# Expert weights in 8 KB rows, and the token rows of six expert pairs fetched by indirect DMA

## The chip, the cores and the metric

The kernel runs on one core of one Trainium2 chip. The metric is device time in microseconds (us). The kernel before has a median of 1703.13 us over three runs (1701.49 to 1704.36).

## The reference

One layer (DEPTH = 1) over 512 latent tokens of width 1024 with 256 context tokens. In fp32 it computes, for `x`:

```python
h = modulate(x, norm1_g, sh_a, sc_a)             # RMSNorm with shift and scale
# three mixers on h: HGRN2 recurrence both ways, gated depthwise conv, grouped-query attention;
# gated projections summed, then w_out
x = x + g_a * y_lat
h = modulate(x, norm2_g, sh_f, sc_f)             # RMSNorm with shift and scale
aff = softmax(h @ router_w)                      # 512 x 16 experts
w_sel, idx = top_k(aff.T, 64)                    # each expert chooses 64 tokens
xs = h[idx]                                      # 16 x 64 x 1024
hid = silu(xs @ w_gate) * (xs @ w_up)            # each expert has 3 weights of 1024 x 1024
ys = (hid @ w_down) * w_sel
x = x + g_f * scatter_add(ys, idx)
out = rmsnorm(x, final_norm_g)
```

The expert weights are 16 x 3 x 4.19 MB, 201 MB in fp32, each read once.

## The kernel before, in words

Up to about 1190 us the kernel computes the mixers, the residual `x1` (four tiles of 128 tokens by 1024) and the router. The change leaves that part alone but for the order of columns in the router and in two small vectors. Attention already runs in program order there; no line of it is in the diff.

The expert stage takes two experts at a time, eight pairs, numbered 0 to 7 here as in the code. `one_hot` (line 1027) makes the 0/1 matrix of a pair: 128 slots, 64 for each expert, over 512 tokens; `ohs` is this matrix with each token's 1/rms (`ss2`) in it. `gather` (line 1039) multiplies `x1` by `ohs` on TensorE, so that the 128 chosen token rows come out transposed and normalised in `xT`, eight column blocks of 128; VectorE and ScalarE apply scale and shift when they evict them. `pair_chunks` (line 1092) multiplies a quarter of a 1024-row weight by the two halves of `xT`, one expert in each half of the partitions. Silu and the product give `hid`; it is transposed to `hT` and multiplied by `w_down`. `weights` (line 1056) fetches each slot's router weight with the same one-hot, `by_slot` (line 1067) transposes the one-hot, and `scatter` (line 1077) adds the results of the pair before to `acc` by matmul.

The order on TensorE is the program's own (a manual schedule). In pair `pr` it is: gate and up chunks of `pr`, gather of `pr + 1`, slot weights, scatter of `pr - 1`, transposes of `hid`, one-hot transposes, down chunks. In pair 0 its own gather stands between the chunks. VectorE, ScalarE and GpSimd are ordered by the planner.

The weights come through SyncE's (SP's) queue in the order of use. A load is one quarter of one expert's matrix, 256 rows of 1024, 1 MB (`wsrc`, line 941); a partition gets two rows that lie 128 rows apart, so two pieces of 4 KB. The last `w_down` pair is loaded by columns instead (`LASTC`), ten loads with pieces of 1 KB or less. The first 24 loads go to 24 slots as these come free; after that the slots are a ring of 20 (`RING`), and load number i waits until TensorE has used load i - 20. `refill` issues what has become possible after each chunk. `early` (line 1103) is the gather of pair 0, two column blocks at a time.

Of the kernel before, what the change touches and what calls it, by code (L numbers as in the profile page):

```python
# [51 lines left out]
def body(tc, x, ctx, cvec, ada_w, ada_b, ada_b0, n1g, n2g, hgn, convw, qg, kg, fng, w_in, w_pa, w_pb, w_pc, w_out,  # L52
# [20 lines left out]
    sc0 = const.tile([128, KC], F32, name="sc0")  # L73
    iota = const.tile([128, 64], F32, name="iota")
    vecs = const.tile([128, 8, 8], F32, name="vecs")
# [94 lines left out]

    last_w = []


# [547 lines left out]

    def column(src, put):
        p = pl.tile([128, KC], F32, name="tp")
        for k in range(KC):
            pe.matmul(p[:, k:k + 1], src[:, k * 128:(k + 1) * 128], ones[:, 0:1], start=True, stop=True)
        put(p)

    def ada_more():

        if not todo:  # L730
            return
        g, k = todo.pop(0)
        w = wraw()
        sp.dma_start(w, ada_w[k * 128:(k + 1) * 128, g * 2048:(g + 1) * 2048])
        if k == 0:
            accs[g] = acp.tile([128, 2048], F32, name="acc")
            ab_r = acp.tile([1, 2048], F32, name="abr")
            act.dma_start(ab_r, ada_b[:, g].rearrange("o j n -> o (j n)"))
            dve.tensor_scalar(accs[g], w, sc0[:, k:k + 1], None, op0=OP.mult)
            dve.tensor_add(accs[g][0:1], accs[g][0:1], ab_r)  # L740
        else:
            dve.scalar_tensor_tensor(accs[g], w, sc0[:, k:k + 1], accs[g], op0=OP.mult, op1=OP.add)
        if k == KC - 1:
            lo, hi = accs[g][:, 0:1024], accs[g][:, 1024:2048]
            if g == 1:
                later.append(lambda: gate_rows(lo))
                later.append(lambda: column(hi, lambda p: dve.tensor_copy(ab2[:, 1], p)))
            else:
                later.append(lambda: column(lo, lambda p: dve.scalar_tensor_tensor(ab2[:, 0], p, 1.0, vecs[:, 1],
                                                                                  op0=OP.add, op1=OP.mult)))  # L750
                later.append(lambda: column(hi, lambda p: dve.tensor_copy(gfc, p)))
# [100 lines left out]
    ss2 = xp.tile([128, 4], F32, name="ss2")  # L852
    aff = xp.tile([128, 4, NE], F32, name="aff")

# [16 lines left out]
    def partial_logits(j2, t):  # L871
        tp = pr_.tile([128, 2, 2, 128], F32, name="tp", bufs=2)
        for kk in range(2):
            for i in range(2):
                pe.transpose(tp[:, kk, i], x1[:, t + i, j2 * 256 + kk * 128:j2 * 256 + kk * 128 + 128], ident)
        xT = wo.tile([128, 2, 2, 128], F32, name="xT", bufs=3)
# [6 lines left out]
    for j2 in range(4):  # L883
# [4 lines left out]
        for t in range(0, 4, 2):  # L888
# [14 lines left out]
            if (j2, t) == (3, 0):  # L903
                preload(ssp[:, 0, 3:4])
    partial_logits(*pend.pop())
    dve.tensor_reduce(ss2, ssp, axis=AX.X, op=OP.add)
    act.activation(ss2, ss2, AF.Sqrt, scale=1.0 / D, bias=eps)
    dve.reciprocal(ss2, ss2)
    pl4 = pr_.tile([128, 4, NE], F32, name="tp", bufs=2)
    for t in range(2):  # L910
# [20 lines left out]
    ma, ma_e = opn("ma", side="right", reuse_waits="tile")  # L931
    wsel = sm.tile([128, NE // 2], F32, name="wsel")
    slot = sm.tile([128, 4, NE], F32, name="slot")
    mx = sm.tile([128, 4], F32, name="rmx")
# [7 lines left out]
    for pr in range(NE // 2):  # L942
        pair = (2 * pr, 2 * pr + 1)
        for kk in range(4):
            for mat in (w_gate, w_up):
                wsrc += [mat[e, kk * 256:kk * 256 + 256].rearrange("(a p) f -> p a f", p=128) for e in pair]
        if pr < NE // 2 - 1:
            for kk in range(4):
                wsrc += [w_down[e, kk * 256:kk * 256 + 256].rearrange("(a p) f -> p a f", p=128) for e in pair]
# [7 lines left out]
    def more(n):  # L957
        for src in wsrc[len(loaded):len(loaded) + n]:
            i = len(loaded)
            name = ORDER[i] if i < len(ORDER) else ring[(i - len(ORDER)) % RING]  # L960
            t = slots[name].tile(list(src.shape), F32, name="mw")
            sp.dma_start(t, src)
            loaded.append(t)

# [58 lines left out]
    pm, pm_e = opn("pm", space=PSUM, bufs=1)  # L1023
    xs = {}
    hot = {}

    def one_hot(pr):
# [5 lines left out]
        dve.tensor_tensor(oh.rearrange("p t (e c) -> p t e c", e=2), slot[:, :, e0:e0 + 2, None].to_broadcast(shape),  # L1033
                          iota[:, None, None, :].to_broadcast(shape), op=OP.is_equal)
        ohs = ma.tile([128, 4, 2 * CAP], F32, name="ohs")
        dve.tensor_mul(ohs, ohf, ss2[:, :, None].to_broadcast([128, 4, 2 * CAP]))
        hot[pr] = oh, ohf, ohs

    def gather(pr, k0, p, on_act):

        ohs = hot[pr][2]
        if pr not in xs:
            xs[pr] = ma.tile([128, KC, 2 * CAP], F32, name="xT")
        xT = xs[pr]
        n = p.shape[1]
        for i in range(n):
            for t in range(4):
                pe.matmul(p[:, i], x1[:, t, (k0 + i) * 128:(k0 + i + 1) * 128], ohs[:, t], start=t == 0, stop=t == 3)  # L1048
        for k in range(k0, k0 + n):
            if on_act:  # L1050
                act.activation(xT[:, k], p[:, k - k0], AF.Identity, scale=ab2[:, 0, k:k + 1], bias=ab2[:, 1, k:k + 1])
            else:
                dve.tensor_scalar(xT[:, k], p[:, k - k0], ab2[:, 0, k:k + 1], ab2[:, 1, k:k + 1], op0=OP.mult,  # L1053
                                  op1=OP.add)

    def weights(pr):

        e0 = 2 * pr
        ohf = hot[pr][1]
        pw = ps.tile([128, NE], F32, name="d")  # L1060
        for t in range(4):
            pe.matmul(pw, ohf[:, t], aff[:, t], start=t == 0, stop=t == 3)
        for e in range(2):
# [39 lines left out]
    def early(k0):  # L1103
        gather(0, k0, ps.tile([128, 2, 128], F32, name="d"), False)

    with tc.manual_schedule(engines={mybir.EngineType.DVE}):
        one_hot(0)
        early(0)
    waiting = None
    for pr in range(NE // 2):  # L1110
# [3 lines left out]
        for kk in range(4):  # L1114
            if kk and pr == 0:
                early(2 * kk)
            for po in (pg, pu):
                pair_chunks(kk, po, xs[pr])
            if pr == 0 and kk == 3:
                one_hot(1)  # L1120
            if last and kk == 0:
                scatter(*waiting, 1, lambda t: ps.tile([128, 1, 512], F32, name="d"))
                weights(pr)
                oT_t = by_slot(pr)
            if last and kk == LATE:
# [20 lines left out]
        if not last and waiting:  # L1146
            scatter(*waiting, 2, lambda t: pm.tile([128, 2, 512], F32, name=("pg", "pu")[t // 2]))
        hT = mb.tile([128, KC, 128], F32, name="hT")
        for h4 in range(2):
            tp = ps.tile([128, 4, 128], F32, name="d")  # L1150
            for i in range(4):
                k = 4 * h4 + i
                pe.transpose(tp[:, i], hid[:, k * 128:(k + 1) * 128], ident)
            act.activation(hT[:, 4 * h4:4 * h4 + 4], tp, AF.Copy)
        if 0 < pr < NE // 2 - 1:
            oT_t = by_slot(pr)
            if pr + 2 < NE // 2:
                one_hot(pr + 2)
        py = pm.tile([128, 2, 512], F32, name="py")
# [4 lines left out]
        if pr == 0:  # L1164
# [13 lines left out]
        waiting = pr, oT_t, yH, yL  # L1178


    sfp = sm.tile([128, 4, len(LASTC)], F32, name="sfp")
    sf = sm.tile([128, 4], F32, name="sf")
# [50 lines left out]
def layout(inp):  # L1233
# [23 lines left out]
    a["w_out"] = f["w_out"][0]  # L1257
    a["router"] = f["router_w"][0].reshape(8, 128, 16).transpose(1, 0, 2)
    a["w_gate"] = f["w_gate"][0]
# [12 lines left out]
    a["sin_d"] = np.sin(ang).astype(np.float32).reshape(4, 128, 32).transpose(1, 0, 2)  # L1272
    a["iota_d"] = np.tile(np.arange(1, 65, dtype=np.float32), (128, 1))
    return {k: np.ascontiguousarray(v) for k, v in a.items()}
# [24 lines left out]
```

## Time and profile before

| | |
|---|---|
| median of three runs | 1703.13 us |
| the profiled execution: its time, its span | 1698.42 us, 1696.6 us |
| TensorE busy (PE) | 1607.2 us, 95% |
| VectorE, ScalarE, GpSimd busy | 767.9, 527.7, 150.7 us |
| moved by DMA | 305.52 MB |
| loads of expert weights | 194 on SP's queue |

The span runs from the first to the last instruction, and the profiled execution's time is 1.8 us longer. PE is TensorE's matmul and PEld its weight load, which overlaps it. A busy PE is not a PE at its peak. The DMA share is the mean busy share of 16 DMA engines; it can exceed 1 a little because packets overlap. For a DMA, the profile gives the issue and the time to landing.

### The profile page before, as it was taken

The numbers are of one execution on the slowest core, as the hardware profiler recorded it, in microseconds if no ns is written. First come the engines' busy times: TensorE is split into PE (matmuls) and PEld (weight loads), VectorE is DVE, ScalarE is ACT, GpSimd is POOL, SyncE is SP. The second block draws the span as 40 slices with busy tenths as digits, with TensorE's granted clock in tenths as the row PEclk, the third lists the DMA queues.
The fourth block names the chain that finished last, engine by engine and source line by source line (L and its number), as shares of the span: only waits on it lengthen the run. The fifth ranks groups of instructions, "written<-read, shape, count | busy, mean of one in ns | idle before, by whom it ended". The sixth has DMA issues, their size and how long they took to land.

```text
span 1696.6 us, 23600 instructions
## 1 busy us (share of the span) xinstructions
PE 1607.2 (95%) x9896; PEld 1207.7 (71%) x9896; DVE 767.9 (45%) x1173; ACT 527.7 (31%) x934; POOL 150.7 (9%) x142
## 2 busy tenths in 40 slices
PE   6999999999998899899999999999799999999996
PEld 4889898988898788788788888889244344444444
DVE  6364655556545666655646524343411222122124
ACT  4433324334225656654323223233010010011004
POOL 0021212222000000000000100110000000000005
PEclk9999999999999999999999999999899999999998
DMA  9410211122222000100555622348789999999995
GB/s 294 118 41 25 63 38 50 38 75 70 80 80 75 26 25 26 44 33 26 182 191 178 209 85 75 124 148 349 315 320 402 382 409 409 409 409 409 409 395 167
DMA packets 166287, 305.52 MB, mean 180 GB/s; under 512 B 6562, under 2 KB 115618, under 8 KB 164130
## 3 DMA queue, kind: packets, MB, share of 16 engines
q1 hardware_dynamic: 162624, 301.66, 48.9%
q10 hardware_dynamic: 3556, 2.35, 0.4%
q8 instruction: 78, 1.28, 0.3%
q14 instruction: 29, 0.24, 0.0%
HBM read 301.89 MB, written 2.10 MB: 179 GB/s over the span
## 4 chain that ended last, share of the span: by engine, by line
PE 83%; DVE 9%; ACT 5%; issue 2%; POOL 0%; DMA 0%; ACTq 0%; SPq 0%; DVEq 0%; POOLq 0%
PE d L185 14%; PE d L187 14%; PE d L186 14%; PE pg L1099 6%; PE pu L1099 6%; PE py L1099 6%; PE py L1048 3%; PE lv L304 2%; PE tp L647 2%; PE tp L632 2%; DVE wl L91 1%; PE mi L333 1%; PE sc L617 1%; PE sc L618 1%; ACT wh L90 1%
## 5 line engine op out<-in xcount | busy, mean ns | idle before, releaser
L185 PE MATMUL d<-hH,wh 128*128 128x512 f32 x640 | 257.2, 402 | 0.0
L187 PE MATMUL d<-hH,wl 128*128 128x512 f32 x640 | 253.4, 396 | 0.0
L186 PE MATMUL d<-hL,wh 128*128 128x512 f32 x640 | 252.4, 394 | 0.0
L91 DVE TENSOR_TENSOR wl<-raw,wh 128x2048 fp32r<-128x2048 f32 (+1 forms) x78 | 157.8, 2022 | 192.0 <-ACT wh L90 191.8
L90 ACT ACTIVATE wh<-raw 128x2048 fp32r<-128x2048 f32 (+1 forms) x78 | 128.9, 1652 | 218.2 <-PE d L186 167.4
L187 PEld LDWEIGHTS d<-hH,wl 128*128 128x128 f32 x640 | 121.0, 189 | 24.9
L185 PEld LDWEIGHTS d<-hH,wh 128*128 128x128 f32 x640 | 120.8, 189 | 22.3 <-issue 1.6
L186 PEld LDWEIGHTS d<-hL,wh 128*128 128x128 f32 x640 | 121.1, 189 | 21.3 <-issue 0.2
L1099 PE MATMUL pg<-mw,xT 128*64 128x512 f32 x512 | 115.6, 593 | 2.0 <-DVE xT L1053 2.0
L1099 PE MATMUL pu<-mw,xT 128*64 128x512 f32 x512 | 115.3, 592 | 0.0
L1099 PE MATMUL py<-mw,hT 128*64 128x512 f32 x448 | 97.7, 594 | 0.1
L315 POOL TENSOR_TENSOR kk<-kk,tt 128x384 f32<-128x384 f32 x56 | 77.0, 1376 | 190.8 <-DVE tt L317 143.6
L1099 PEld LDWEIGHTS pu<-mw,xT 128*64 128x64 f32 x512 | 36.7, 137 | 73.1 <-issue 72.8
L1099 PEld LDWEIGHTS pg<-mw,xT 128*64 128x64 f32 x512 | 36.1, 137 | 72.2 <-issue 68.8
L185 PE MATMUL d<-wh,hH 128*128 128x256 f32 x288 | 84.1, 292 | 0.0
L187 PE MATMUL d<-wh,hL 128*128 128x256 f32 x288 | 81.7, 284 | 0.0
L186 PE MATMUL d<-wl,hH 128*128 128x256 f32 x288 | 81.6, 283 | 0.0
L1140 DVE TENSOR_TENSOR hid<-hid,pu 128x1024 f32<-128x1024 f32 x8 | 9.8, 1221 | 154.4 <-PE pu L1099 148.0
L187 PE MATMUL d<-brh,wl 128*128 128x512 f32 x192 | 75.6, 396 | 2.6 <-DVE wl L91 2.6
L185 PE MATMUL d<-brh,wh 128*128 128x512 f32 x192 | 75.8, 396 | 1.7 <-ACT wh L90 1.5
L186 PE MATMUL d<-brl,wh 128*128 128x512 f32 x192 | 75.7, 396 | 0.0
L1099 PEld LDWEIGHTS py<-mw,hT 128*64 128x64 f32 x448 | 31.5, 137 | 60.8 <-issue 59.7
(354 smaller groups left out, 2998.1 us busy)
## 6 DMA issues: line engine op xcount, KB each, us to landing
mw<-in_w_gate_dram SPq DMA_DIRECT2D x64, 1024.0 KB, 18.2
mw<-in_w_up_dram SPq DMA_DIRECT2D x64, 1024.0 KB, 18.5
mw<-in_w_down_dram SPq DMA_DIRECT2D x62, 1024.0 KB, 17.4
raw<-in_w_in_dram SPq DMA_DIRECT2D x38, 1024.0 KB, 5.1
raw<-in_ada_w_dram SPq DMA_DIRECT2D x16, 1024.0 KB, 4.9
raw<-in_w_in_dram SPq DMA_DIRECT2D x24, 512.0 KB, 3.8
adaw<-in_ada_w_dram SPq DMA_DIRECT2D x8, 512.0 KB, 8.5
raw<-in_ada_w_dram SPq DMA_DIRECT2D x8, 512.0 KB, 7.8
```

What stands on the lines that cost most here:

```text
L90: act.activation(hi, src, AF.Copy)
L91: dve.tensor_sub(lo, src, hi)
L185: pe.matmul(p, lh(k), rh(k), start=k == 0, stop=False)
L186: pe.matmul(p, lh(k), rl(k), start=False, stop=False)
L187: pe.matmul(p, ll(k), rh(k), start=False, stop=k == KC - 1)
L304: pe.matmul(p[:, c], kc[:, c * 128:(c + 1) * 128], q_mix, start=True, stop=True)
L315: pool.tensor_mul(kb[:, :, 1], kb[:, :, 1], tb[:, :, 0, 0:1].to_broadcast([128, n2, m]))
L333: pe.matmul(pv[:, i], kt[:, i], v[:, c], start=True, stop=True)
L632: pe.transpose(tp[:, t], e[:, (t0 + t) * 128:(t0 + t + 1) * 128], ident)
L647: pe.matmul(av[hh * 64:hh * 64 + 64, i], va[:, t, g * 64:g * 64 + 64], pts[hh][:, t], start=t == 0, stop=t == 5)
L1048: pe.matmul(p[:, i], x1[:, t, (k0 + i) * 128:(k0 + i + 1) * 128], ohs[:, t], start=t == 0, stop=t == 3)
L1099: pe.matmul(dst[64 * e:64 * e + 64, hf_], src[:, k, 64 * e:64 * e + 64], wt[e][:, k2, hf_ * 512:hf_ * 512 + 512], start=k == 0, stop=k == ...
```

## The change

- **Weight loads.** A quarter's 256 rows are laid out so that partition p gets rows 2p and 2p + 1, which follow each other in memory: one piece of 8 KB instead of two of 4 KB. The pieces of the last `w_down` pair stay.
- **Order of columns.** With that layout a column block of a weight's rows holds every second row of 256. All that meets them is permuted to match by `every2`: the gather, the transposes of `hid` (but for the last pair), the router's transposes, the modulation vectors, `norm2_g` and the router weight.
- **Token rows.** `x1` is stored to a DRAM buffer `xd` by four DMAs on SP. From pair 2 on the gather by matmul is gone. `weights` now also multiplies the one-hot by the token's number and its 1/rms (`facts`), and so yields the index of each slot's token (`which`) and its 1/rms (`norm`). `fetch` reads the 128 rows from `xd` with an indirect DMA on GpSimd's queue and scales them on VectorE. `turn_rows` transposes them in eight blocks on TensorE and evicts them half on VectorE, half on ScalarE.
- **Order.** In pair `pr` TensorE now does: gate and up chunks, `turn_rows(pr + 1)`, slot weights of `pr + 2`, transposes of `hid`, scatter of `pr - 1`, one-hot transposes of `pr + 1`, down chunks. Pairs 0 and 1 keep the gather. `fetch(pr + 2)` comes at the end of pair `pr`; `fetch(2)` after the first chunks of pair 1. The fetched rows, `hid` and `yt` share one buffer.

```diff
+    def every2(v, k):
+
+        o = k // 2 * 256 + k % 2
+        return v[:, o:o + 255:2]
...
+    facts = xp.tile([128, 4, NE + 2], F32, name="aff")
+    aff = facts[:, :, :NE]
+    dram, dram_e = opn("xd", space=bass.MemoryType.DRAM)
+    xd = dram.tile([S, D], F32, name="xd")
...
+    for t in range(4):
+        sp.dma_start(xd[t * 128:(t + 1) * 128], x1[:, t])
...
+    pool.tensor_copy(facts[:, :, NE:NE + 1], iota[:, 64:68, None])
+    pool.tensor_copy(facts[:, :, NE + 1:NE + 2], ss2[:, :, None])
...
-                wsrc += [mat[e, kk * 256:kk * 256 + 256].rearrange("(a p) f -> p a f", p=128) for e in pair]
+                wsrc += [mat[e, kk * 256:kk * 256 + 256].rearrange("(p a) f -> p (a f)", p=128) for e in pair]
...
+            if len(src.shape) == 2:
+                t = t.rearrange("p (a f) -> p a f", a=2)
...
+    def evict(xT, p, k, on_act):
+        if on_act:
+            act.activation(xT[:, k], p, AF.Identity, scale=ab2[:, 0, k:k + 1], bias=ab2[:, 1, k:k + 1])
+        else:
+            dve.tensor_scalar(xT[:, k], p, ab2[:, 0, k:k + 1], ab2[:, 1, k:k + 1], op0=OP.mult, op1=OP.add)
+
+    def pick(pr, k0, p, on_act):
+
+        xT, ohs = xs[pr]
         n = p.shape[1]
         for i in range(n):
             for t in range(4):
+                pe.matmul(p[:, i], every2(x1[:, t], k0 + i), ohs[:, t], start=t == 0, stop=t == 3)
+        for i in range(n):
+            evict(xT, p[:, i], k0 + i, on_act)
+
+    def fetch(pr):
+
+        xg = mb.tile([128, D], F32, name="hid")
+        pool.indirect_dma_start(xg, None, xd, bass.IndirectOffsetOnAxis(ap=which.pop(pr), axis=0))
+        dve.tensor_scalar(xg, xg, norm[:, pr:pr + 1], None, op0=OP.mult)
+        fetched[pr] = xg
+
+    def turn_rows(pr):
+
+        xg = fetched.pop(pr)
+        p = pm.tile([128, 2, 4, 128], F32, name="py")
+        xT = ma.tile([128, KC, 2 * CAP], F32, name="xT")
+        for k in range(KC):
+            pe.transpose(p[:, k // 4, k % 4], every2(xg, k), ident)
+        for k in range(4):
+            evict(xT, p[:, 0, k], k, False)
+            evict(xT, p[:, 1, k], k + 4, True)
+        xs[pr] = xT, None
 
     def weights(pr):
 
         e0 = 2 * pr
         ohf = hot[pr][1]
+        pw = ps.tile([128, NE + 2], F32, name="d")
         for t in range(4):
+            pe.matmul(pw, ohf[:, t], facts[:, t], start=t == 0, stop=t == 3)
+        if pr > 1:
+            which[pr] = sm.tile([128, 1], mybir.dt.uint32, name="which", bufs=2)
+            dve.tensor_copy(which[pr], pw[:, NE:NE + 1])
+            dve.tensor_copy(norm[:, pr:pr + 1], pw[:, NE + 1:NE + 2])
...
-                pair_chunks(kk, po, xs[pr])
+                pair_chunks(kk, po, xs[pr][0])
             if pr == 0 and kk == 3:
                 one_hot(1)
+            if pr == 1 and kk == 0:
+                weights(2)
+                fetch(2)
             if last and kk == 0:
                 scatter(*waiting, 1, lambda t: ps.tile([128, 1, 512], F32, name="d"))
-                weights(pr)
-                oT_t = by_slot(pr)
...
+        if 0 < pr and not last:
+            turn_rows(pr + 1)
         hid = mb.tile([128, D], F32, name="hid")
         act.activation(hid, pg.rearrange("p a b -> p (a b)"), AF.Silu)
         dve.tensor_mul(hid, hid, pu.rearrange("p a b -> p (a b)"))
-        if not last:
+        if pr == 0:
+            scaled(1)
             pn = pm.tile([128, 2, 4, 128], F32, name="py")
-            gather(pr + 1, 0, pn[:, 0], False)
-            gather(pr + 1, 4, pn[:, 1], True)
-            weights(pr)
-        if not last and waiting:
-            scatter(*waiting, 2, lambda t: pm.tile([128, 2, 512], F32, name=("pg", "pu")[t // 2]))
+            pick(1, 0, pn[:, 0], False)
+            pick(1, 4, pn[:, 1], True)
+            weights(0)
+            weights(1)
+        elif pr + 2 < NE // 2:
+            weights(pr + 2)
         hT = mb.tile([128, KC, 128], F32, name="hT")
         for h4 in range(2):
             tp = ps.tile([128, 4, 128], F32, name="d")
             for i in range(4):
                 k = 4 * h4 + i
-                pe.transpose(tp[:, i], hid[:, k * 128:(k + 1) * 128], ident)
+                pe.transpose(tp[:, i], (hid[:, k * 128:(k + 1) * 128] if last else every2(hid, k)), ident)
             act.activation(hT[:, 4 * h4:4 * h4 + 4], tp, AF.Copy)
-        if 0 < pr < NE // 2 - 1:
-            oT_t = by_slot(pr)
-            if pr + 2 < NE // 2:
-                one_hot(pr + 2)
+        if not last and waiting:
+            scatter(*waiting, 2, lambda t: pm.tile([128, 2, 512], F32, name=("pg", "pu")[t // 2]))
+            turned[pr + 1] = by_slot(pr + 1)
+            if pr + 3 < NE // 2:
+                one_hot(pr + 3)
...
-            oT_t = by_slot(0)
+            for i in range(2):
+                turned[i] = by_slot(i)
             one_hot(2)
+            one_hot(3)
...
-
+        waiting = pr, turned.pop(pr), yH, yL
+        if 0 < pr < NE // 2 - 2:
+            fetch(pr + 2)
```

## Rows read from the trace of the kernel before

**Rows 1.** The page's slices, 40 of 42.4 us each; busy tenths of TensorE and DMA.

```profile
PE   6999999999998899899999999999799999999996
...
DMA  9410211122222000100555622348789999999995
```

**Rows 2.** Chain of waits, pair 4 and on; start us, us, what.

```profile
1449.38 3.43 PE pg L1099 x16
...
1476.85 3.78 PE py L1048 x32
...
1480.66 1.38 DVE xT L1053 x4
...
1485.92 0.80 PE d L1062 x8
...
1506.91 1.28 PE pg L1099 x5
```

**Rows 3.** Stretches; busy us (count) by engine, granted clock, DMA share, GB/s.

```profile
1334.00:1622.00 288.00, 277.43 (x1464) 129.61 (x1462) 57.79 (x84) 27.20 (x50) 0.00 (x0) 1.00 1.03 409
...
1400.00:1410.00 10.00, 10.00 (x50) 3.29 (x48) 0.00 (x0) 0.00 (x0) 0.00 (x0) 1.00 1.02 408
...
749.50:751.50 2.00, 2.00 (x20) 1.51 (x20) 1.37 (x2) 0.89 (x4) 0.00 (x0) 1.00 0.96 397
...
883.20:885.20 2.00, 2.00 (x11) 1.65 (x10) 0.00 (x0) 0.51 (x1) 0.00 (x0) 1.00 0.88 348
...
1213.50:1266.30 52.80, 49.16 (x288) 25.92 (x288) 6.40 (x16) 4.84 (x8) 0.00 (x0) 1.00 0.76 299
...
813.00:820.00 7.00, 4.12 (x17) 2.66 (x15) 7.00 (x8) 4.84 (x7) 0.00 (x0) 0.99 0.42 137
...
820.00:826.50 6.50, 5.29 (x13) 4.12 (x14) 3.45 (x2) 1.91 (x1) 0.00 (x0) 0.50 0.53 179
```

**Rows 4.** Loads' issue (start us, us) and DMA view (KB, us to landing).

```profile
1222.37 0.88 SPq L962 DMA_DIRECT2D mw<-in_w_up_dram  x2
...
mw<-in_w_up_dram SPq DMA_DIRECT2D x1, 1024.0 KB, 6.6
...
1566.73 2.31 SPq L962 DMA_DIRECT2D mw<-in_w_up_dram  x1
...
mw<-in_w_up_dram SPq DMA_DIRECT2D x1, 1024.0 KB, 18.5
...
1664.83 1.23 SPq L962 DMA_DIRECT2D mw<-in_w_down_dram  x1
...
mw<-in_w_down_dram SPq DMA_DIRECT2D x1, 512.0 KB, 6.5
```

**Rows 5.** TensorE in order of time; start us, us, line, operation, out<-in.

```profile
1222.28 2.05 PE L1048 MATMUL d<-ohs,x 128*128 128x128 f32 x16
...
1280.05 3.60 PE L1099 MATMUL pu<-mw,xT 128*64 128x512 f32 x16
...
1491.21 1.03 PE L1153 MATMUL d<-ident,hid 128*128 128x128 f32 x8
...
1588.30 3.60 PE L1099 MATMUL pu<-mw,xT 128*64 128x512 f32 x16
...
1680.49 1.97 PE L1194 MATMUL pg<-mw,hT 128*64 128x128 f32 x32
```

**Rows 6.** Lines 1139 and 1140; duration ns min/median/max.

```profile
L1139 ACT ACTIVATE hid<-pg x8: 1023/1023/1026, 1249.0 to 1657.8; 128x1024 f32<-128x1024 f32 x8
...
L1140 DVE TENSOR_TENSOR hid<-hid,pu x8: 1220/1220/1222, 1251.2 to 1661.9; 128x1024 f32<-128x1024 f32 x8
```

**Rows 7.** DMA issues; KB each, median us to landing.

```profile
out_dram<-moe SPq DMA_DIRECT2D x4, 512.0 KB, 3.4
```

**Rows 8.** Line 304; duration ns min/median/max.

```profile
L304 PE MATMUL lv<-qq,kc x448: 270/275/414, 82.3 to 423.9; 128*128 128x128 f32 x150
```

**Rows 9.** Groups of line 1048, 1213 to 1250; busy us, mean ns.

```profile
L1048 PEld LDWEIGHTS d<-ohs,x 128*128 128x128 f32 x62 | 7.2, 192 | 2.4 <-issue 2.4
```

More of the change, by code (lines that the diff above doesn't have):

```diff
@@ L73, in body @@
     sc0 = const.tile([128, KC], F32, name="sc0")
-    iota = const.tile([128, 64], F32, name="iota")
+    iota = const.tile([128, 68], F32, name="iota")
     vecs = const.tile([128, 8, 8], F32, name="vecs")
@@ L720, in body, with column @@
     accs = {}
-    def column(src, put):
+    def column(src, put, at_k=lambda v, k: v[:, k * 128:(k + 1) * 128]):
         p = pl.tile([128, KC], F32, name="tp")
         for k in range(KC):
-            pe.matmul(p[:, k:k + 1], src[:, k * 128:(k + 1) * 128], ones[:, 0:1], start=True, stop=True)
+            pe.matmul(p[:, k:k + 1], at_k(src, k), ones[:, 0:1], start=True, stop=True)
         put(p)
@@ L746, in ada_more @@
                 later.append(lambda: gate_rows(lo))
-                later.append(lambda: column(hi, lambda p: dve.tensor_copy(ab2[:, 1], p)))
+                later.append(lambda: column(hi, lambda p: dve.tensor_copy(ab2[:, 1], p), every2))
             else:
                 later.append(lambda: column(lo, lambda p: dve.scalar_tensor_tensor(ab2[:, 0], p, 1.0, vecs[:, 1],
-                                                                                  op0=OP.add, op1=OP.mult)))
+                                                                                  op0=OP.add, op1=OP.mult), every2))
                 later.append(lambda: column(hi, lambda p: dve.tensor_copy(gfc, p)))
@@ L852, in body @@
     ss2 = xp.tile([128, 4], F32, name="ss2")
-    aff = xp.tile([128, 4, NE], F32, name="aff")
+    facts = xp.tile([128, 4, NE + 2], F32, name="aff")
+    aff = facts[:, :, :NE]
+    dram, dram_e = opn("xd", space=bass.MemoryType.DRAM)
+    xd = dram.tile([S, D], F32, name="xd")
     ra = wo.tile([128, KC, 32], F32, name="ra")
@@ L874, in partial_logits @@
             for i in range(2):
-                pe.transpose(tp[:, kk, i], x1[:, t + i, j2 * 256 + kk * 128:j2 * 256 + kk * 128 + 128], ident)
+                pe.transpose(tp[:, kk, i], every2(x1[:, t + i], 2 * j2 + kk), ident)
         xT = wo.tile([128, 2, 2, 128], F32, name="xT", bufs=3)
@@ L932, in body @@
     wsel = sm.tile([128, NE // 2], F32, name="wsel")
+    norm = sm.tile([128, NE // 2], F32, name="norm")
     slot = sm.tile([128, 4, NE], F32, name="slot")
@@ L945, in body @@
             for mat in (w_gate, w_up):
-                wsrc += [mat[e, kk * 256:kk * 256 + 256].rearrange("(a p) f -> p a f", p=128) for e in pair]
+                wsrc += [mat[e, kk * 256:kk * 256 + 256].rearrange("(p a) f -> p (a f)", p=128) for e in pair]
         if pr < NE // 2 - 1:
             for kk in range(4):
-                wsrc += [w_down[e, kk * 256:kk * 256 + 256].rearrange("(a p) f -> p a f", p=128) for e in pair]
+                wsrc += [w_down[e, kk * 256:kk * 256 + 256].rearrange("(p a) f -> p (a f)", p=128) for e in pair]
         else:
@@ L1023, in body @@
     pm, pm_e = opn("pm", space=PSUM, bufs=1)
-    xs = {}
-    hot = {}
+    xs, hot, which, fetched = {}, {}, {}, {}
     def one_hot(pr):
@@ L1033, in one_hot, with scaled @@
         dve.tensor_tensor(oh.rearrange("p t (e c) -> p t e c", e=2), slot[:, :, e0:e0 + 2, None].to_broadcast(shape),
-                          iota[:, None, None, :].to_broadcast(shape), op=OP.is_equal)
+                          iota[:, None, None, 0:64].to_broadcast(shape), op=OP.is_equal)
+        hot[pr] = oh, ohf
+    def scaled(pr):
         ohs = ma.tile([128, 4, 2 * CAP], F32, name="ohs")
[L1036 to L1044, printed above, removed]
+        dve.tensor_mul(ohs, hot[pr][1], ss2[:, :, None].to_broadcast([128, 4, 2 * CAP]))
+        xs[pr] = ma.tile([128, KC, 2 * CAP], F32, name="xT"), ohs
+    def evict(xT, p, k, on_act):
[5 more added lines that the diff above has]
+        xT, ohs = xs[pr]
         n = p.shape[1]
@@ L1047, in gather @@
             for t in range(4):
[L1048 to L1054, printed above, removed]
+                pe.matmul(p[:, i], every2(x1[:, t], k0 + i), ohs[:, t], start=t == 0, stop=t == 3)
[16 more added lines that the diff above has]
+        xs[pr] = xT, None
     def weights(pr):
@@ L1059, in weights @@
         ohf = hot[pr][1]
-        pw = ps.tile([128, NE], F32, name="d")
+        pw = ps.tile([128, NE + 2], F32, name="d")
         for t in range(4):
-            pe.matmul(pw, ohf[:, t], aff[:, t], start=t == 0, stop=t == 3)
+            pe.matmul(pw, ohf[:, t], facts[:, t], start=t == 0, stop=t == 3)
[3 more added lines that the diff above has]
+            dve.tensor_copy(norm[:, pr:pr + 1], pw[:, NE + 1:NE + 2])
         for e in range(2):
@@ L1103, in early @@
     def early(k0):
-        gather(0, k0, ps.tile([128, 2, 128], F32, name="d"), False)
+        pick(0, k0, ps.tile([128, 2, 128], F32, name="d"), False)
     with tc.manual_schedule(engines={mybir.EngineType.DVE}):
         one_hot(0)
+        scaled(0)
         early(0)
+    turned = {}
     waiting = None
@@ L1177, in body @@
             split(yH[:, sl], yL[hf_], yt[:, sl])
-        waiting = pr, oT_t, yH, yL
+        waiting = pr, turned.pop(pr), yH, yL
+        if 0 < pr < NE // 2 - 2:
+            fetch(pr + 2)
+    oT_t = turned.pop(pr)
     sfp = sm.tile([128, 4, len(LASTC)], F32, name="sfp")
@@ L1246, in layout @@
     a["n1g"] = pp(f["norm1_g"][0])
-    a["n2g"] = pp(f["norm2_g"][0])
+    a["n2g"] = f["norm2_g"][0].reshape(4, 128, 2).transpose(1, 0, 2).reshape(128, 8)
     a["hgn"] = pp(f["hg_norm_g"][0])
@@ L1257, in layout @@
     a["w_out"] = f["w_out"][0]
-    a["router"] = f["router_w"][0].reshape(8, 128, 16).transpose(1, 0, 2)
+    a["router"] = f["router_w"][0].reshape(4, 128, 2, 16).transpose(1, 0, 2, 3).reshape(128, 8, 16)
     a["w_gate"] = f["w_gate"][0]
@@ L1272, in layout @@
     a["sin_d"] = np.sin(ang).astype(np.float32).reshape(4, 128, 32).transpose(1, 0, 2)
-    a["iota_d"] = np.tile(np.arange(1, 65, dtype=np.float32), (128, 1))
+    a["iota_d"] = np.concatenate([np.tile(np.arange(1, 65), (128, 1)), np.arange(512).reshape(4, 128).T],
+                                 axis=1).astype(np.float32)
     return {k: np.ascontiguousarray(v) for k, v in a.items()}
```

## The prediction

> **What bounds the kernel now.** I read the page's slices first [rows 1]. Up to slice 26 TensorE is busy eight or nine tenths and the DMA engines six at most after the start. From slice 31 on both stand at nine: TensorE at full clock, the DMA at 409 GB/s. So in the expert stage two resources are nearly equal, and the question is which one ends last.
>
> The chain of waits of one expert pair [rows 2] answers for TensorE. The stage is TensorE work end to end, and a pair takes 1506.91 - 1449.38 = 57.53 us. Of this the two gather halves with the wait between them take from 1476.85 to 1485.92, that is 9.07 us.
>
> The stretches [rows 3] answer for the DMA. From 1334 to 1622 it moves 409 GB/s at a share of 1.03: no gap is left. A pair loads 24 tiles of 1.0486 MB, 25.17 MB, which is 61.5 us at 409 GB/s. So the DMA is 4 us per pair slower than TensorE and lives on a lead.
>
> Issue, landing and first use show that lead [rows 4, 5]. The load issued at 1222.37 lands 6.6 us later, at 1229.0, and is used at 1280.05: 51 us early. The one issued at 1566.73 lands 18.5 us later, at 1585.2, and is used at 1588.30: 3 us early. The last load, of a tile half as large, is issued at 1664.83, lands at 1671.3 and is used at 1680.49: 9.2 us early, since the last pair has extra TensorE work. So TensorE sets the end today, but with 3 to 9 us of cover. What is taken from TensorE beyond that falls to the DMA. This is why I count the change in DMA time.
>
> **The gather leaves TensorE.** Pairs 2 to 7 lose the 64 gather instructions, 9.07 us each [rows 2], six times: 54.4 us. In their place come eight transposes of fetched rows, as many as the eight of `hid`, 1.03 us [rows 5]. New wait: fetched rows, `hid` and `yt` share one buffer, so Silu (1.02 us) and the product (1.22 us) [rows 6] start only after these transposes. TensorE meanwhile has the slot weights (0.80 us, [rows 2]), then idles about 1.5 us. If four ACT evictions go ahead of Silu it is some 1.4 us more, by the four that stand as one piece of 1.38 us [rows 2]. Queued behind that wait are `hid`'s transposes, the scatter and the down matmuls. A pair costs TensorE 57.53 - 9.07 + 1.03 + 1.5 to 3 = 51 to 52.5 us. TensorE alone would end 30 to 39 us earlier, at 1658 to 1667. That is not the time, because the DMA is late next: the lead of 51 us, less at each pair's end, goes by 8 to 10 us per pair (61.5 - 52.5 to 51 or so), and from about pair 4 or 5 on TensorE waits for weights.
>
> **The weight rows.** 184 of the 194 loads change from two 4 KB pieces per partition to one of 8 KB; the last ten keep their short rows. Bytes stay. What one busy DMA engine moves I take as GB/s over share. The 4 KB stream gives 408/1.02 = 400 and 409/1.03 = 397. The only 8 KB rows of this trace, lone 1 MB loads of `ada_w`, give 397/0.96 = 414 at best and 348/0.88 = 395 at worst [rows 3]. A lone burst has ragged ends, a stream none, so I take the good one: 414/400 = 1.034, with bounds 395/400 = 0.99 and 414/397 = 1.042. About 40 loads are in by 1266, so 144 remain in the stretch without gaps: 151 MB, 369.2 us at 409 GB/s, 357.1 us at 423. That is -12.1 us (bounds +3.7 and -14.9).
>
> One rule speaks against this. The Trainium skill ("DMA: Bandwidth & Descriptors", "Where 436 GB/s comes from") says that for HBM to SBUF the memory side binds at about 358 GB/s; with a bound there, row length would be worth nothing and the term would be 0 instead of -12.1. The stream at 409 GB/s in [rows 3] already exceeds that figure, so this case does not bear it out as a ceiling; a memory bound near 409 is still open and is a rival below.
>
> **The fetched rows.** Six indirect DMAs of 128 rows of 4 KB add 3.15 MB to the same DMA engines; at 409 GB/s that is 1.28 us each, +7.7 us. The trace has no indirect DMA. Below nothing they can't be, since nothing is loaded less. Above I take the 3.4 us in which a plain 512 KB transfer lands [rows 7], as if the stream stood still for it: 20.4 us. I take 7.7: the fetched pieces are as long as those of the stream, whose row is the nearest. Their latency is hidden: a fetch is issued at a pair's end (the first, of pair 2, after the first block of pair 1) and needed after the next 27 us of gate and up matmuls. VectorE's scaling of the rows waits for the landing, and one-hot work and evictions queue behind it, but nothing there is needed before the pair's end.
>
> **The edits that I cost at nothing.** The four stores of x1 (2.1 MB, 5.1 us at 409 GB/s) stand on SP's queue among the first 24 loads and wait there for x1; what is behind them lands about that much later. From 1213.5 to 1266.3 the DMA's share is 0.76 [rows 3]: nearly 13 us of idle time take this up. Without that cover it would be 5 us. The two `facts` copies run on POOL, which is free there. The permuted columns change addresses, not counts: stationary operands are now read with a step of two. No row shows a stepped stationary operand. Below nothing it can't go; above, doubled weight loads are a rival. The nearest row, line 304, whose moving operand is stepped at seven different scales, has 270 to 275 ns at minimum and median [rows 8], so I take nothing. The Trainium skill ("SBUF — State Buffer", "Specifications (TRN2)") says that an SBUF read keeps full rate as long as two accesses fall in one 16-byte line, which a step of two fp32 does; by it the term is also 0, and no run here shows it for weights. The scatter that moves behind `hid`'s transposes keeps its count. One block of slot weights moves into pair 0, +0.8 us, where releases of ring tiles pace the loads (share 0.76 from 1213.5 to 1266.3 [rows 3]), so it counts.
>
> **The sum.** Last landing: 1671.3 - 12.1 + 7.7 + 0.8 = 1667.7. TensorE waits for it instead of the reverse: the lead of 9.2 us is gone, and of the block before, 1.97 us long like the last [rows 5], I count some 1.4 us still to do when it lands. From the use of the last load to the end 1696.6 - 1680.49 = 16.1 us stay [rows 5]. End: 1667.7 + 1.4 + 16.1 = 1685.2, 11.4 us under the span of 1696.6. The profiled execution took 1698.42, 1.8 more than its span, so 1687.0; the median of the runs, 1703.13, is 4.7 above the profiled one, so 1691.7.
>
> **Rivals.**
> - Row length brings nothing: the stream is held at 409 GB/s by the memory. For it: the steadiness of 408 to 409 in every stretch. Against: the 8 KB bursts. 1691.7 + 12.1 = 1703.8, no change, although TensorE lost 54 us of work.
> - The fetches are dear, at 3.4 us each: +12.7, so 1704.4; again no change.
> - Slower: the stepped stationary operand doubles the weight load. It decides in pairs 0 and 1, where the gather stays on TensorE. Sixteen instructions take 2.05 us there [rows 5], and their weight loads, 192 ns each, are busy for nearly all of it (62 for 7.2 us, [rows 9]), so doubled loads would double the 128 instructions' 16 us. Ring releases pace the DMA there, so all of it counts: 1691.7 + 16 = 1707.7. Slower than before from 11.4 us on, that is at some 220 ns per instruction instead of 125. Against it: line 304.
> - TensorE's clock falls in the waits. After 820 the granted clock is 0.50, the 1.2 GHz level, behind a stretch with 4.12 of 7.00 us busy [rows 3]. Waiting for weights, TensorE would be busy 3.43 us [rows 2] in each 4.96 (2.1 MB at 423 GB/s), much the same. A fall in the middle lets the loads get ahead and is paid back; at the end it costs one such stretch of 6.5 us, half of it: 1695.
>
> **How the numbers follow.** Forecast 0.64, alone 1686 to 1698. Row length nothing 0.12, fetches dear 0.06, stepped loads 0.12, clock 0.06. The range reaches down to 1683 (rows at 1.042 and a small loss elsewhere) and up to 1705, which takes in both cases without change and leaves out most of the slower one. A change under 0.2% (3.4 us) can't be told from none. Faster: 0.64 + 0.06 = 0.70; same: 0.12 + 0.06, less a little, 0.17; slower 0.13.
>
> **What would show it.** DMA at 420 to 425 GB/s in the expert stage: the row length. At 409: the first rival. TensorE idle before the expert matmuls with a weight DMA as releaser, some 20 to 30 us in all, from pair 4 or 5 on, and a last load used 1 to 2 us after it lands: the bound has changed hands. Pairs 2 and 3 of about 52 us and later ones of about 61: both limits. Gather weight loads at 192 ns in pair 0: no cost of the step. I am wrong if TensorE does not wait for the DMA at the end, if the last pairs still run at 57 us, or if the time before the expert stage moves by more than 3 us.

## The result and the profile after

The changed kernel takes 1691.82 us (median of four runs, 1690.92 to 1692.93) where the kernel before, run beside it, takes 1702.77: a ratio of 0.9936 [0.9918, 0.9953], 10.9 us less. The profiled execution took 1692.65 us, its span 1690.9.

The page's slices, TensorE (PE) and the DMA engines in 40 equal parts of the span; the rows of before are [rows 1]:

```profile
PE   6999999999998899899999999999799999989796
DMA  9320112112222000010554622327988999999997
GB/s 293 99 63 26 55 34 63 34 55 75 76 88 92 26 26 26 26 51 27 174 195 155 211 90 97 125 89 309 383 362 356 412 420 419 419 419 419 420 414 227
```

The DMA engines are full from slice 32 on (before: from 31), now at 412 to 420 GB/s. TensorE, which stood at nine tenths there, drops to eight and seven in slices 36 and 38. The stretches say the same and show two more things that come up below (times from the span's start; busy us of PE, PEld, DVE, ACT and POOL with instruction counts, granted clock, DMA share, GB/s; before in [rows 3]):

```profile
1334.00:1622.00 288.00, 261.74 (x1220) 104.19 (x1216) 62.25 (x95) 29.56 (x52) 4.69 (x5) 0.99 1.01 419
1213.50:1266.30 52.80, 48.61 (x281) 26.81 (x280) 8.76 (x22) 4.04 (x7) 0.00 (x0) 1.00 0.95 389
...
1417.00:1423.00 6.00, 4.20 (x31) 3.17 (x28) 2.69 (x8) 1.83 (x3) 0.00 (x0) 1.00 1.02 422
1423.00:1426.40 3.40, 3.40 (x11) 2.50 (x10) 1.75 (x3) 0.92 (x2) 0.00 (x0) 0.51 1.01 419
```

What TensorE waited for from 1210 us on (total us, number of waits, longest):

```profile
PE d L1201 <- DVE hid L1186: 13.3, 7, 2.4
PE pu L1140 <- DMA mw<-in_w_up_dram: 7.4, 5, 2.1
PE pg L1140 <- DMA mw<-in_w_gate_dram: 5.1, 4, 1.3
```

In the kernel before no expert matmul waited for a weight. Now nine do, for 12.5 us, and one more (0.6 us) in the last block. Where it happens is seen in TensorE's order of work in pair 5 (start, us, operation, idle before and its releaser):

```profile
1502.50 3.60 PE L1140 MATMUL pg<-mw,xT 128*64 128x512 f32 x16
...
1511.52 3.22 PE L1140 MATMUL pg<-mw,xT 128*64 128x512 f32 x13 [1.12 <-DMA mw<-in_w_gate_dram]
...
1516.50 3.22 PE L1140 MATMUL pu<-mw,xT 128*64 128x512 f32 x13 [1.33 <-DMA mw<-in_w_up_dram]
...
1526.46 3.65 PE L1140 MATMUL pu<-mw,xT 128*64 128x512 f32 x14 [1.33 <-DMA mw<-in_w_up_dram]
1530.04 1.22 PE L1087 MATMUL py<-ident,hid 128*128 128x128 f32 x8
...
1533.87 1.23 PE L1201 MATMUL d<-ident,hid 128*128 128x128 f32 x8 [1.80 <-DVE hid L1186]
```

A chunk of 3.4 us of matmul starts each 5 us, as the loads land. The gather's nine microseconds [rows 2] are gone; eight transposes of fetched rows (line 1087, 1.22 us) stand in their place. The chain of waits jumps to the loads at this place, one behind another, and comes back to TensorE in pair 6:

```profile
1499.24 3.43 PE pu L1140 x16
1502.67 3.25 PE pg L1140 x15
1505.92 20.50 DMA mw<-in_w_up_dram
...
1526.48 20.11 DMA mw<-in_w_down_dram
1546.66 21.16 DMA mw<-in_w_up_dram
1567.89 19.87 DMA mw<-in_w_up_dram
...
1587.80 3.65 PE pu L1140 x14
```

I measure the expert stage from its first gate matmul to the end of the span, because the time ahead of it differs between executions of one kernel: it starts at 1216.6 us in one execution of a kernel of the experiments (rows_only) and at 1220.2 in another. A period is the distance between the first gate matmuls of two pairs.

| kernel | stage starts | stage, us | periods of pairs 0 to 6, us | TensorE's waits for weights, us |
|---|---|---|---|---|
| before | 1215.3 | 481.3 | 61.3 57.6 57.5 57.5 57.5 57.5 57.5 | 0 |
| after | 1218.8 | 472.1 | 63.2 55.3 53.3 53.2 51.9 58.7 61.2 | 13.1 |
| after, once more | 1220.6 | 471.1 | 63.2 54.7 53.1 53.1 53.2 58.5 62.3 | 11.1 |

Pairs 2 to 4 show one bound, TensorE with less work; pairs 5 and 6 the other, the weights: 25.17 MB of loads at 419 GB/s are 60.1 us, with a fetch of 0.52 MB 61.3. The last up chunk of pair 5 starts at 1526.46 and that of pair 6 at 1587.80: 61.3 us apart.

### The profile page after: what moved, and what is told of

Same layout as the page of the kernel before. It is cut to its first block, busy times and chain, and to the rows that moved or that the text cites. A ratio compares the mean times of both kernels' runs of the same rounds, so it can differ in the third digit from the quotient of the medians.

```text
span 1690.9 us, 22958 instructions
## 1 busy us (share of the span) xinstructions
PE 1585.1 (94%) x9560; PEld 1180.1 (70%) x9560; DVE 770.0 (46%) x1185; ACT 529.4 (31%) x934; POOL 157.0 (9%) x150
## 4 chain that ended last, share of the span: by engine, by line
PE 79%; DVE 7%; DMA 6%; ACT 5%; issue 2%; POOL 0%; SPq 0%; ACTq 0%; DVEq 0%; POOLq 0%
PE d L190 14%; PE d L192 14%; PE d L191 14%; PE pg L1140 5%; PE pu L1140 5%; PE py L1140 5%; DMA mw<-in_w_up_dram 4%; PE lv L309 2%; PE tp L652 2%; PE tp L637 2%; DMA mw<-in_w_down_dram 2%; PE mi L338 1%; DVE wl L91 1%; PE sc L622 1%; PE sc L623 1%
## 5 line engine op out<-in xcount | busy, mean ns | idle before, releaser
L1140 PE MATMUL pu<-mw,xT 128*64 128x512 f32 x512 | 121.0, 593 | 7.4 <-DMA mw<-in_w_up_dram 7.4
L1140 PE MATMUL pg<-mw,xT 128*64 128x512 f32 x512 | 120.4, 595 | 7.1 <-DMA mw<-in_w_gate_dram 5.1
L637 PE MATMUL tp<-ident,e 128*128 128x128 f32 x384 | 56.7, 276 | 18.5 <-ACT pt L641 11.6
L628 ACT ACTIVATE e<-sc,mx 128x768 f32<-128x768 f32 x64 | 57.7, 902 | 52.0 <-DVE mx L626 51.7
```

What stands on the lines that cost most here:

```text
L628: act.activation(e, pf, AF.Exp, bias=mx, accum_out=dens[g, hp][:, qt, hh:hh + 1])
L637: pe.transpose(tp[:, t], e[:, (t0 + t) * 128:(t0 + t + 1) * 128], ident)
L1140: pe.matmul(dst[64 * e:64 * e + 64, hf_], src[:, k, 64 * e:64 * e + 64], wt[e][:, k2, hf_ * 512:hf_ * 512 + 512], start=k == 0, stop=k == ...
```

## The experiments

Ten runs followed, eight of new kernels, one of the changed kernel again and one of `rows_only` again (`rows_only_b`). The theory: the fetch takes work from TensorE until the weight stream is the bound, and the 8 KB rows pay because that stream is then the bound. The rivals were that the fetches cost more or less than their bytes, that the step of two costs time, and that TensorE still sets the end. All medians stand beside the kernel before on the same chip (1701.37 for the first four, 1701.32 for the next four, 1700.24 for the last two). `short_rows`, `fetch_thin` and `fetch_twice` are compared below with `after_again`, which ran on another chip; the kernel before is within 0.1 us on the two.

| run | median, us | ratio to before | stage, us | waits for weights, us |
|---|---|---|---|---|
| short_rows | 1698.64 | 0.9980 [0.9969, 0.9991] | 479.3 | 19.8 |
| rows_only | 1706.80 | 1.0030 [1.0018, 1.0042] | 486.0 | 0 |
| fetch_thin | 1688.81 | 0.9919 [0.9903, 0.9936] | 467.1 | 6.8 |
| fetch_twice | 1698.80 | 0.9987 [0.9974, 1.0000] | 480.1 | 16.1 |
| after_again | 1691.51 | 0.9944 [0.9931, 0.9957] | 471.1 | 11.1 |
| more_turns | 1705.74 | 1.0026 [1.0015, 1.0037] | 487.2 | 0 |
| mix247 | 1689.53 | 0.9934 [0.9921, 0.9946] | 473.6 | 0 |
| mix2347 | 1688.41 | 0.9926 [0.9913, 0.9939] | 468.7 | 1.9 |
| rows_nostep | 1702.70 | 1.0008 [0.9997, 1.0019] | 482.6 | 0 |
| rows_only_b | 1704.34 | 1.0027 [1.0014, 1.0040] | 484.6 | 0 |

### The fetch without the 8 KB rows

```diff
-        o = k // 2 * 256 + k % 2
-        return v[:, o:o + 255:2]
+        return v[:, k * 128:(k + 1) * 128]
...
-rearrange("(p a) f -> p (a f)", p=128)
+rearrange("(a p) f -> p a f", p=128)
```

(The norm2_g and router layouts are those of before as well.)

> The changed kernel with the weights back in two 4 KB pieces per partition and the column order undone; indirect fetch and TensorE order as changed. Stream theory (the end of the weight stream sets the time, 8 KB rows shorten it by about 10 to 12 us): 1702 to 1704, the same as the kernel before, the stream at 409 GB/s, TensorE idle for weights 20 us or more. Relief theory (the gain comes from the gather that left TensorE): 1690 to 1693, as with the change.

Measured 1698.64 us, between the numbers of the two theories and nearer to the stream's. The stream runs at the old rate:

```profile
1400.00:1500.00 100.00, 93.66 (x434) 38.67 (x432) 22.97 (x36) 10.71 (x20) 0.94 (x1) 0.97 1.03 409
```

Against the whole change (after_again, 1691.51) the short rows cost 7.1 us by the medians, 6.1 by the ratios to before and 8.2 by the stage. TensorE waits 19.8 us for weights instead of 11.1. So the row length is worth 6 to 8 us here, not 12. This kernel also reads without the step of two, which makes its TensorE a little faster; the step is taken apart below.

### The 8 KB rows without the fetch

The kernel before, with the loads of two adjoining rows and the permuted columns in the gather, the transposes of `hid`, the router and the two vectors:

```diff
-[mat[e, kk * 256:kk * 256 + 256].rearrange("(a p) f -> p a f", p=128) for e in pair]
+[mat[e, kk * 256:kk * 256 + 256].rearrange("(p a) f -> p (a f)", p=128) for e in pair]
...
-                pe.matmul(p[:, i], x1[:, t, (k0 + i) * 128:(k0 + i + 1) * 128], ohs[:, t], start=t == 0, stop=t == 3)
+                pe.matmul(p[:, i], every2(x1[:, t], k0 + i), ohs[:, t], start=t == 0, stop=t == 3)
```

> The kernel before with 8 KB rows and the column order that goes with them, gather by matmul in all pairs, no fetch. Stream theory: TensorE sets the end here at 57.5 us per pair, so the time stays within 3 us of the kernel before (1700 to 1706), while the last load lands about 10 us earlier against its use than before. Rival (row length alone gives the gain): 1690 to 1693.

> The rows_only kernel again, beside the run before on one chip: both theories 1705 to 1708.

Measured 1706.80 and 1704.34, slower than before by 0.3% in both, the first 0.8 us above the range given for it, the second 0.7 us below. The loads come sooner and nobody needs them sooner: the last one lands at 1668.3 and is used at 1690.1, 22 us later. Each period is 58.0 us instead of 57.5. The groups of the gather's and the transposes' weight loads (busy us, mean ns, idle before):

```profile
L1054 PEld LDWEIGHTS py<-ohs,x 128*128 128x128 f32 x448 | 53.8, 196 | 17.2 <-DVE xT L1059 11.6 <-issue 5.7
...
L1159 PEld LDWEIGHTS d<-ident,hid 128*128 128x128 f32 x64 | 9.1, 204 | 3.4 <-DVE hid L1146 2.8
```

### The same, with the step of two taken out

This kernel reads unpermuted columns in the gather and in the router's and `hid`'s transposes; one of the three edits:

```diff
-                pe.matmul(p[:, i], every2(x1[:, t], k0 + i), ohs[:, t], start=t == 0, stop=t == 3)
+                pe.matmul(p[:, i], x1[:, t, (k0 + i) * 128:(k0 + i + 1) * 128], ohs[:, t], start=t == 0, stop=t == 3)
```

> The rows_only kernel with its gather, the transposes of hid and the router's transposes reading unstepped column blocks again, while weights and vectors keep the new order: blocks meet rows that are not theirs, so the expert results are left wrong and only the time counts. Theory that the stepped stationary operands make rows_only slower than the kernel before (gather weight loads 196 instead of 192 ns, transposes about 208 instead of 140, some 0.5 us per pair): 1700 to 1703, as the kernel before. Rival (the 8 KB loads themselves delay something): 1705 to 1708, as rows_only.

Measured 1702.70, on one chip with 1704.34 for the stepped one. The periods are back at 57.5 us, and the same two groups nearly at their old means (192 and 142 ns before):

```profile
L1054 PEld LDWEIGHTS py<-ohs,x 128*128 128x128 f32 x448 | 51.1, 192 | 17.2 <-DVE xT L1059 11.6 <-issue 5.7
...
L1159 PEld LDWEIGHTS d<-ident,hid 128*128 128x128 f32 x64 | 7.9, 150 | 3.9 <-DVE hid L1146 2.8 <-PE d L1159 0.2
```

The step costs a gather load 4 to 5 ns and a transpose's load 54 to 62 ns, and a pair 0.4 us where TensorE is the bound (pair 0: 0.7): 1.6 us in the medians, whose intervals overlap a little, 2.0 in the stage, 3.3 by seven periods. The periods are the clean figure: in the last pair the profiled execution of rows_nostep has a fall of TensorE's granted clock to 0.50 for 3.4 us (from 1669.6), that of rows_only_b and that of before have none, and from the last pair's first gate matmul to the end they take 76.0, 74.7 and 74.7 us. What is left of rows_only's loss, 2.5 us from before to rows_nostep on that chip, is not explained by the step, and may be nothing: the interval of rows_nostep holds no change.

### Less and more to fetch

`fetch_thin` fetches 128 columns of each row and takes the other 896 from a fixed block of `x1`, copied on GpSimd; `fetch_twice` fetches all rows twice into the same buffer.

```diff
-        pool.indirect_dma_start(xg, None, xd, bass.IndirectOffsetOnAxis(ap=which.pop(pr), axis=0))
+        pool.indirect_dma_start(xg[:, 0:128], None, xn, bass.IndirectOffsetOnAxis(ap=which.pop(pr), axis=0))
+        pool.tensor_copy(xg[:, 128:], x1[:, 0, 128:])
```

> The changed kernel, but each fetch reads 512 bytes of a row instead of 4 KB; the other seven eighths of the fetched tile are filled with a copy of other rows by GpSimd, so that part of the gather is left out. 2.75 MB less goes through the DMA engines. Stream theory: 6 to 7 us less than the changed kernel, 1684 to 1687. Rival (fetches fill gaps of the stream and cost nothing): 1690 to 1693.

```diff
+        at = which.pop(pr)
+        for _ in range(2):
+            pool.indirect_dma_start(xg, None, xd, bass.IndirectOffsetOnAxis(ap=at, axis=0))
```

> The changed kernel with every indirect fetch made twice into the same tile: 3.15 MB more. Stream theory with 1.28 us per fetch: 7 to 9 us more than the changed kernel, about 1699 to 1701. Fetches at 3.4 us each: 1712. Fetches in gaps: 1690 to 1693.

Twice costs 7.3 us over after_again by the medians (8.0 to 8.9 by the stage): 1.2 to 1.5 us per fetch of 0.52 MB, the time of its bytes. Thin gives back only 2.7 us by the medians, 4 to 5 by the stage, less than the six or seven I expected. One likely reason is that the first fetches fall partly into time that the stream leaves free. Thin's stretch around pair 1 is not full:

```profile
1290.00:1334.00 44.00, 41.37 (x198) 18.42 (x196) 9.72 (x19) 4.43 (x8) 1.94 (x2) 0.96 0.97 397
```

Its stage starts 2.6 us after that of after_again and 4.5 after that of after, so the comparison has to go by the time from the stage's start: from 100 to 120 us after it thin moves 391 GB/s at a share of 0.98, after_again 417 and after 408, both at 1.01. That is 0.3 to 0.5 MB, about the bytes of one thinned fetch. And with the stream relieved, TensorE (6.8 us of waits left) is nearer to being the bound. How the rest divides between the two is not shown.

### The change once more, and more work for TensorE

> The changed kernel once more, as the neighbour of the three below on one chip. All theories: 10 to 12 us under the kernel before.

It repeats the result: 1691.51. Beside it ran the kernel with the eight transposes of `turn_rows` made six times, 40 more per pair:

```diff
+        for _ in range(5):
+            for k in range(KC):
+                pe.transpose(p[:, k // 4, k % 4], every2(xg, k), ident)
```

> The changed kernel with the eight transposes of the fetched rows done six times over, 40 more per pair in pairs 2 to 7, about 5.7 us of TensorE each and 34 us in all; the result is the same. Stream theory: TensorE waits for weights anyway, at most 5 us more than the changed kernel. Relief theory (TensorE's time sets the end): 25 to 34 us more.

The chain of waits of its pair 5 (start, us, what) shows the price, and a clock effect to which I come back:

```profile
1541.62 3.43 PE pu L1143 x16
1545.06 1.16 PE py L1087 x8
1546.21 4.80 PE py L1090 x40
...
1553.62 1.36 PE d L1204 x8
1554.97 0.43 PE pg L1129
1555.40 0.43 PE pg L1130
```

Measured 1705.74, 14.2 us over after_again (16.1 by the stage); both theories' numbers missed. Six times 4.80 us are 28.8 us, so 14.6 of them (12.7 by the stage) vanished into waits that were there. No wait for weights is left, and the periods from pair 2 on are 57.9 to 58.1 us: TensorE is the bound again. So the bound had moved, but the room on TensorE was only 13 to 15 us. Without the added transposes its own stage would be, by estimate, 487.2 - 28.8 = 458.4 us, 22.9 under before and 13.7 under after.

### Fetching for some pairs only

If both resources are nearly level, fewer fetches should do as well. Both kernels gather by matmul again in the pairs that `FETCH` does not list.

```diff
+FETCH = (2, 3, 4, 7)
...
-        if 0 < pr and not last:
+        if pr + 1 in FETCH:
             turn_rows(pr + 1)
...
-        if pr == 0:
-            scaled(1)
+        if not last and pr + 1 not in FETCH:
+            scaled(pr + 1)
```

> The changed kernel with the fetch for pairs 2, 4 and 7 only; pairs 3, 5 and 6 gather by matmul again. Stream theory: three fetches less take 3.9 us from the stream, and three gathers put some 16 to 20 us on TensorE, which is about what it waits or has as lead: 2 to 4 us less than the changed kernel, unless TensorE becomes the bound again. Relief theory: 12 to 16 us more.

> As the run before, with the fetch for pairs 2, 3, 4 and 7. Stream theory: two fetches less, 2 to 3 us less than the changed kernel. Relief theory: 8 to 11 us more.

With three fetches (2, 4, 7) 1689.53 us, with four 1688.41, the best of all; where six took 1691.51 on the same chip. The intervals of four [0.9913, 0.9939] and six [0.9931, 0.9957] overlap a little, so that four beat six by 3.1 us is likely and not settled, though each of the five executions with four was faster than each of the five with six. Three do no worse than six. The relief theory, 8 to 16 us more, is refuted; the stream theory's numbers, 2 to 4 and 2 to 3 us less, are nearly met (2.0 and 3.1). What TensorE waited for with four:

```profile
PE d L1204 <- DVE hid L1188: 9.6, 5, 2.4
PE py L1071 <- DVE xT L1063: 4.4, 3, 1.5
...
PE pu L1141 <- DMA mw<-in_w_up_dram: 1.9, 2, 1.3
```

1.9 us of waiting for weights, and a stream that still carries 419 GB/s from 1334 to 1622 us: neither of the two has much room.

## Why the prediction was right

**The bound changed hands.** Right. The waits for weights begin in pair 5; the periods go from about 53 to 58.7 and 61.2. Both edits were needed for it: the rows alone cost 0.3%, the fetch alone gains 0.2%, both together 0.6%. The rows speed up a transfer that nobody waits for until the fetch makes TensorE wait for it. I had also said that TensorE would wait for the last load. It hardly does: its waits for weights lie in pairs 5 and 6, and after the last up chunk of pair 6 the changed kernel has one wait of 0.6 us for a weight, and after_again has none. The last load still lands about 1 us before its use.

**The sum, from the start of the stage.** I forecast a last landing 3.6 us earlier (-12.1 + 7.7 + 0.8) and a lead cut from 9.2 to 1.4 us, so -11.4. The use of the last load comes at 1674.79 against 1680.49 [rows 5], and the stage began 3.5 us later: -9.2. The next to last landing is at 1672.2. It follows the ones at 1668.7 and 1670.4 in steps of 1.8 us: these loads have short pieces, and the DMA moves 350 GB/s and less there, not 419. So the last should land at 1674.0 (an estimate; the trace has no landing for it). The lead is then some 0.8 us, and the landing, counted from the stage's start, -0.9 us instead of -3.6. The timeline of the issue of the next to last load and of the use of the last (start, us), and that load's landing, 7.9 us after issue:

```profile
1664.31 2.58 SPq L976 DMA_DIRECT2D mw<-in_w_down_dram  x1
...
1674.79 1.97 PE L1248 MATMUL pg<-mw,hT 128*64 128x128 f32 x32
```

```profile
mw<-in_w_down_dram SPq DMA_DIRECT2D x1, 512.0 KB, 7.9
```

From the use to the end it is 16.1 us, as before.

**The rate of the rows** is the term that was mis-sized. I took 423 GB/s from one lone burst [rows 3]; the stream makes 419: 369.2 us times (1 - 409/419) = 8.8 us instead of 12.1, and 6.1 to 8.2 by short_rows. The rival "row length brings nothing" is refuted. The Trainium skill ("DMA: Bandwidth & Descriptors", "Where 436 GB/s comes from") puts the memory's bound at some 358 GB/s for a transfer from HBM to SBUF; the 419 GB/s of this stream decide against it as a ceiling here.

**The fetches** cost their bytes, as taken: 7.7 us forecast, 7.3 measured by fetch_twice. "Dear fetches" is refuted. They land 8.8 us after issue (median of six), well ahead of the next need, which is a pair's gate and up matmuls later:

```profile
hid<-xd,which POOLq DMA_INDIRECT x6, 8.8
xd<-x SPq DMA_DIRECT2D x4, 512.0 KB, 3.4
```

**The stores of `x1`** cost nothing that shows. They delayed the loads behind them on SP's queue, issued at 1184.81 and from 1191.82 us on, 25 us and more later than the same loads in the kernel before; but the DMA's share from 1213.5 to 1266.3 rose from 0.76 [rows 3] to 0.95: the cover I named was used. Over the profiled executions the stage starts between 1215.3 and 1221.5 us without the stores and between 1216.3 and 1223.2 with them. No run leaves out the stores alone, or the new place of the scatter alone.

**The step of two** was costed at nothing and is not free. The gather's and the transposes' weight loads in the changed kernel (ns least/median/most, first and last start):

```profile
L1070 PEld LDWEIGHTS d<-ohs,x x64: 192/196/197, 1216.1 to 1246.9; 128*128 128x128 f32 x64
...
L1201 PEld LDWEIGHTS d<-ident,hid x64: 138/209/260, 1265.8 to 1656.2; 128*128 128x128 f32 x64
```

196 ns against the 192 of [rows 9] is far from doubled, so the slower rival fails. The transposes' loads go from 140 to 209 ns (medians); there are 16 such transposes in a pair with a fetch, and in pairs 5 and 6, where TensorE waits for weights, their cost takes nothing from the end. The Trainium skill ("SBUF — State Buffer", "Specifications (TRN2)") gives full rate as long as two accesses fall in one 16-byte line; the gather's 4 ns come near it, the transposes' 69 ns do not agree.

**The cover of TensorE** was overestimated. I had TensorE alone ending 30 to 39 us earlier; more_turns shows 22.9. Waits for weights came to 11 to 13 us, not 20 to 30. The work in a pair was right: pair 4, with neither a wait for weights nor a fall of the clock, takes 51.9 us, where I had 51 to 52.5, and the new wait for `hid`, 1.5 to 3 us forecast, is 13.3 us in seven pairs, at most 2.4. What the sum lacked is the clock: with a fall, which each of pairs 1 to 7 has in more_turns, a fetched pair takes 53.3 us (58.1 - 4.8), 1.4 more. Pair 0 takes 1.9 us more than before instead of 0.8; rows_only shows 0.7 of that as the step's. Seven falls and pair 0 are some 12 us (an estimate), which would bring 22.9 back into the range. The shortfall did not move the end much, because TensorE's waits for the weights took it up.

**Two slips in the working** decided nothing. The 1.38 us of four evictions [rows 2] are VectorE's and not ScalarE's, and 61.5 less 51 to 52.5 is 9 to 10.5 us per pair, not 8 to 10.

**The offset.** My span was 5.7 us too low (1685.2 against 1690.9): 3.5 of it before the stage, past the 3 us that I had named as the mark of error, and 2.2 in it. That the median came out within 0.2 us is partly luck. I added 6.5 us from span to median, since before's profiled execution was faster than its runs; after's median is only 0.9 above its span. The two errors cancel. The time ahead of the stage is not the change's doing so far as the runs tell: over all profiled executions the stage starts between 1215.3 and 1223.2 us, and two of the same kernel differ by 3.6. The last section shows what it goes with.

## What to carry to other kernels

When two resources are nearly level, work taken from one pays only up to the lead of the other, and an edit that helps the second alone can even cost; try the two together, and then give back part of the first until neither waits (four fetches of six here). Double a suspected cost and add work to the engine that should be free: both give the price and the room directly. Compare stages from their own start, since the time ahead of them may differ more between executions than the edit is worth.

## What was not expected of the hardware

TensorE's granted clock fell at the ends of pairs. In the profiled execution of before it stays at full from 1202 to 1687 us; after the change it is 0.50 to 0.51, the 1.2 GHz level, for 3.4 us in the stretch from 1423.00 shown above, and likewise at 1313.8 (for 6.8 us) and 1368.4 (3.4). Just before, TensorE was busy 4.20 of 6.00 us, in the waits for `hid`; the scatter that follows then runs at 0.43 us a matmul instead of 0.23. The chain of after through this place and through the next pair's end, which has no fall:

```profile
1423.14 0.40 PE pg L1126
1423.54 0.43 PE pg L1127
1423.97 0.43 PE pg L1126
...
1476.35 0.24 PE pg L1126
1476.59 0.23 PE pg L1127
1476.82 0.23 PE pg L1126
```

A fall costs some 1.6 us of TensorE (eight matmuls, 0.2 us each), about the difference between the period of pair 4, 51.9 us and without a fall, and those of pairs 2 and 3, 53.3 and 53.2. In fetch_twice it is pairs 2 and 3 that have no fall, and they take 51.9 us. In more_turns, where TensorE is the bound, the row at 1554.97 shows it too. The last rival, the clock, was thus right about the fall, though in another place. In this execution all three falls lie ahead of the waits for weights, which take up what they cost; after_again has one more from 1596.5 us on, behind its last such wait, with no later one to take it up. Whether another order of `hid`'s work would avoid it was not tried.

Falls of different length also stand ahead of the stage. Those of before and after in the program's first microseconds and behind the router:

```profile
24.60:31.40 6.80, 4.75 (x25) 2.22 (x25) 5.44 (x9) 3.20 (x4) 0.00 (x0) 0.50 1.22 291
1191.80:1202.30 10.50, 3.88 (x8) 0.89 (x9) 8.24 (x21) 0.26 (x1) 0.25 (x8) 0.51 1.03 414
```

```profile
27.00:37.20 10.20, 10.01 (x57) 6.51 (x47) 5.49 (x11) 1.77 (x3) 0.00 (x0) 0.50 1.19 288
1194.30:1208.00 13.70, 6.91 (x12) 1.30 (x12) 11.05 (x27) 0.26 (x1) 0.48 (x9) 0.50 1.01 411
```

After's are 3.4 and 3.2 us longer. At half speed that is worth up to 1.7 and 1.6 us, which together could make up nearly all of the 3.5 us by which its stage starts later. The twelve profiled executions bear it out. In the five with 31 to 38 us at half clock ahead of the stage, before among them, it starts at 1215.3 to 1216.8 us; in the seven with 41 to 48 us, after among them, at 1218.8 to 1223.2. The whole time goes with the granted clock too: of the twelve executions of rows_only_b, the seven with a mean clock of 0.986 or more took 1702.5 to 1705.2 us, the five with 0.982 to 0.984 1707.0 to 1710.1. What makes a fall longer in one execution than in another stays open.
